# A two-layer decoder trunk on one core: keys times -1/8, attention parts at higher priority and further apart, the second half's row factors spread in one piece

## The chip, the cores and the metric

The kernel runs on one core of a Trainium2 chip. The metric is device time in microseconds (us), the median of several executions; lower is better. In the profile, PE is the engine of matmuls (TensorE) and PEld its weight loads, which overlap the matmuls; DVE (VectorE) does elementwise work and row reductions, ACT (ScalarE) activations and copies out of PSUM, POOL (GpSimd) further elementwise work, and SP issues the DMAs.

## The reference

One sequence of 1024 tokens, width 1024, goes through two layers. Layer 0 mixes by sliding-window attention, layer 1 by a gated recurrence (HGRN2); each layer has one wide input projection, a gate, an output projection and a norm on either side. The change concerns layer 0:

```python
h = rmsnorm(x, pre_norm_w)
q, k, v, z = split(h @ w_in + b_in, [1024, 1152, 1280])   # 16 query heads, 2 key heads, 64 wide
q, k = partial_rope(q), partial_rope(k)                   # rotates the first 16 of 64
# blocks of 128 queries against their own and the previous 128 keys:
s = einsum('bqhgd,bkhd->bhgqk', qi, ki) * 64 ** -0.5
s = where(valid, s, -inf)                                  # causal, at most 128 keys back
m = maximum(max(s, axis=-1), sink)                         # one learned sink per head
p = exp(s - m)
p = p / (sum(p, axis=-1) + exp(sink - m))
o = einsum('bhgqk,bkhd->bqhgd', p, v)
x = x + rmsnorm((o * silu(z)) @ w_out + b_out, post_norm_w)
```

## The kernel before

**Projections.** Every projection is computed as a sum of three matmuls: activations and weights are each split into a high part and the rest (the tiles `acth`/`actl` and `whi`/`wlo`), and `product` (L214) issues high times high, high times low and low times high, 128x512 each, into one PSUM tile. Eight products make a *unit*: 128 output columns for 512 tokens (`proj_feat`, L228). A weight piece arrives by DMA in `wraw`; POOL or ACT makes `whi` from it and DVE makes `wlo` (L179). There are ten places for split pieces, and one comes free when all its products are issued.

**What sets the order.** The products are the clock of the program: `later(d, f)` (L223) puts a piece of other work into a plan, to be issued d products from now, and `product` issues what is due. During attention, PE's instructions are kept in exactly this program order. The order on DVE, ACT, POOL and SP is chosen by a scheduler, from its own estimate of when operands are ready and from priorities: within `hp()` an instruction counts as 400 places earlier in the program than it stands. Each engine then runs its list strictly from front to back.

**Start.** Keys and values of token half 0, and the first query units, are computed before the normed activations exist in full: rows are scaled afterwards by factors that are turned into a 128x512 tile (`rb0`, `rb1`) by four PE transposes and one ACT copy (`spread`, tile `psr`). `first_scaled` does this for half 0 within the third unit (`ps2`), after its product 4. For half 1, `spread(rs1, rb1)` follows the fourth unit (`ps3`), then `q_unit(0, 0, 0)` projects and rotates the last query unit of half 0. `scaled_half` multiplies the second half's input `xt` by `rb1` (DVE) and splits it into `acth`/`actl`.

**Attention.** There are 32 steps, counted from 0: 2 key heads (g) x 8 blocks (b) x 2 (`par`, which four of the eight heads). Each step has three parts, put into the plan by the loop under `A0, AP, AT, AV = 25, 7.3, 11, 21`: step i's `scores` at product 25 + 7.3 i, its `turned` 11 products later, its `heads_out` 21 products later. The parts are called by `at_once`, within `hp()`. A step's chain through the engines is:

- `scores`: PE multiplies queries (`QS`, fetched by a DMA from DRAM) and keys (`KH`, `KL`) into two PSUM tiles `pss`; ACT copies the always-valid part to `sm` (L690), DVE copies the masked part over it with a predicate (L694, twice); column 129 of `sm` holds 8 times the sink. DVE takes each row's maximum (L698) into `st` and multiplies it by -1/8 (L699); ACT makes four exponentials (L701) with that as the bias and 1/8 as the scale, summing each row; DVE makes the reciprocals (L703) and scales `sm` by them (L704).
- `turned`: PE transposes `sm` in four matmuls (tile `pst`); ACT copies the high part to `pT` (L713), DVE makes the low part (L714), POOL zeroes what is outside the window (L720 to L728).
- `heads_out`: PE multiplies by the values (tile `pso`); ACT and DVE evict (L746, L747), and for g = 1 DVE multiplies into the gated tile `og` (L749).

Between these parts PE works off the list `fill`: the key unit of half 1, the value unit of half 1, the query units `q_unit(0, ct, 1)`, eight units `q_unit(1, ct, half)`, sixteen gate units (`z_unit`) and four units of the output projection. A query unit with `ct` = 0 is rotated (*rope*) with DVE operations at L423 to L425 and L427, the others take L430; both write a single-buffered tile `ql`, which a DMA moves to `qd` in DRAM. Before the output projection, `g_split` (L775) splits `og` for token half 0: ACT at L780, DVE at L781, the first four of the eight pieces in one go.

Of the kernel before, what the change touches and what calls it, by code (L numbers as in the profile page):

```python
# [27 lines left out]
NH = 16  # L28
HD = 64
EPS = 1e-6  # L30
NEG = -1.0e30


INV_FREQ = [float.fromhex(h) for h in (
# [55 lines left out]
def emit(tc, I, out):  # L90
# [9 lines left out]
    with top:  # L100
# [122 lines left out]
        def later(d, f, block=99):  # L223

            W["plan"].append((W["pos"] + d, f, block))
            W["plan"].sort(key=lambda e: e[0])

        def proj_feat(first, half, tag="mm", then={}):  # L228

            ps = mm(tag=tag)  # L230
            for k in range(NK):
                c = (k % 4) * P
                product(ps, k, weight(first, k // 4, c, c + P), act[k, half])
                used(first + k // 4)
                then.get(k, lambda: None)()
            return ps
# [48 lines left out]
        def bias(i):  # L285
            return cst[:, C_BIN + i:C_BIN + i + 1]
# [86 lines left out]
        def layer0():  # L373
# [26 lines left out]
            def q_first(g, ct):  # L400
                return 12 + 2 * ct if g else 2 * ct if ct else 8
# [35 lines left out]
            with pool("start", "right") as sp:  # L437
# [41 lines left out]
                with tc.high_priority(offset=1000):  # L479
# [50 lines left out]
                            sc.append(vsc if i == 0 else qp.tile([P, 512], F32, tag="th", bufs=2, name="sc"))  # L530
                            v.tensor_tensor(sc[i], first[i], rb0, op=ALU.mult)

                    ps2 = proj_feat(q_first(0, 2), 0, "s", {4: first_scaled})
                    split_next()
                    rs1 = [row_rstd(sp, rows[1][j], jkb) for j in range(4)]
                    cs3 = sines()
# [2 lines left out]
                    split_next()  # L539
                    ps3 = proj_feat(q_first(0, 3), 0, "s")  # L540
                    rb1 = sp.tile([P, 512], F32, name="rb1")
                    spread(rs1, rb1)
                    advance(W_K + 2)
                    for e in heads:
                        e.on = False
# [1 line left out]
                def k_unit(half):  # L547
                    cs = slice(half * 512, (half + 1) * 512)
                    ps = proj_feat(W_K, half)
                    with hp():  # L550
                        ps = scaled(ps, half)
                        kr = qp.tile([P, 512], F32, tag="th", bufs=2, name="kr") if half else ps
                        nc.scalar.activation(kr, ps, AF.Identity, bias=bias(0))
                    v.tensor_tensor(kf, kr, cosK[:, cs], op=ALU.mult)
                    for o in range(4):
                        s1, s2 = slice(32 * o, 32 * o + 8), slice(32 * (o ^ 1), 32 * (o ^ 1) + 8)
                        s3 = slice(64 * (o % 2), 64 * (o % 2) + 8)
                        v.tensor_tensor(tK[s1], kr[s2], sinT[s3, cs], op=ALU.mult)
                    v.tensor_tensor(kf, kf, tK, op=ALU.add)

                    def halves(kv):
                        kr = kf[64 * kv:64 * kv + 64]
                        for o in (0, 64):
                            nc.scalar.activation(KH[o:o + 64, kv, cs], kr, AF.Copy)
                            v.tensor_tensor(KL[o:o + 64, kv, cs], kr, KH[o:o + 64, kv, cs].bitcast(F32), op=ALU.subtract)

                    for kv in range(2):
                        if half:
                            def behind(kv):

                                with tc.issue_after(W["exp"].ins):
                                    halves(kv)
                            later(30 + 6 * kv, lambda kv=kv: behind(kv))
                        else:
                            halves(kv)

                def v_unit(half, ps=None, sc=None):
# [34 lines left out]
                        rest(VL, pl.rearrange("p (k d) -> p k d", k=2))  # L612

                    if half:
                        later(4, turned)
                        later(6, last_turned)
                    else:
                        turned()

# [1 line left out]
                q_unit(0, 1, 0, first[1], 0, sc[1])  # L621
                q_unit(0, 2, 0, ps2, 2)
                for_keys()
                nc.gpsimd.tensor_scalar(hbias, cst[:, C_BIN:C_BIN + 18], 0.5, 1.0, op0=ALU.mult, op1=ALU.mult)
                q_unit(0, 3, 0, ps3, 4)
                scaled_half(xt1, rb1, 1)
                q_unit(0, 0, 0, at=6)
                second_tables()
                k_unit(0)

            with pool("att", "right") as ap:
# [35 lines left out]
                def scores(g, b, par):  # L667
# [3 lines left out]
                    if par == 1 and (g, b) != order[-1]:  # L671
                        queries(*order[order.index((g, b)) + 1])
                    QS = QSs[g, b]

                    sms[g, b, par] = sm = ap.tile([P, 4, P + 1], F32, tag="sm", bufs=2, name="sm")
                    nc.gpsimd.tensor_scalar(sm[:, :, P:], cst[:, C_SINK + 8 * g + par:C_SINK + 8 * g + 8:2].unsqueeze(2),
                                            8.0, 1.0, op0=ALU.mult, op1=ALU.mult)
                    if b == 0:
                        nc.gpsimd.memset(sm[:, :, :P], NEG)
                    k0 = max(b - 1, 0) * P  # L680
                    nkk = (b + 1) * P - k0
                    for hp in range(2):
# [12 lines left out]
                                          mk.rearrange("p (u c) -> p u c", c=64).unsqueeze(1).to_broadcast([P, 2, 2, 64]), src)  # L695
                    st = ap.tile([P, 3, 4], F32, tag="st", bufs=4, name="st")
                    nm, dn, rd = (st[:, i, :] for i in range(3))
                    v.tensor_reduce(nm, sm, axis=AX.X, op=ALU.max)  # L698
                    v.tensor_scalar(nm, nm, -0.125, None, op0=ALU.mult)  # L699
                    for h in range(4):  # L700
                        W["exp"] = nc.scalar.activation(sm[:, h, :], sm[:, h, :], AF.Exp, bias=nm[:, h:h + 1], scale=0.125,  # L701
                                                        accum_out=dn[:, h:h + 1])
                    v.reciprocal(rd, dn)  # L703
                    v.tensor_tensor(sm[:, :, :P], sm[:, :, :P], rd.unsqueeze(2).to_broadcast([P, 4, P]), op=ALU.mult)  # L704
# [56 lines left out]
                order = [(g, b) for g in range(2) for b in range(8)]  # L761

                def at_once(f, *a):
                    with hp():
                        f(*a)


                A0, AP, AT, AV = 25, 7.3, 11, 21
                W["pos"] = 0
                for i, (g, b, par) in enumerate((g, b, par) for g, b in order for par in range(2)):  # L770
                    for d, f in ((0, scores), (AT, turned), (AV, heads_out)):
# [474 lines left out]
```

## Time and profile before

| what | value |
|---|---|
| time, median of 3 runs | 916.68 us (914.98 to 917.44) |
| time of the profiled execution | 916.49 us |
| its span (first to last instruction) | 914.8 us |
| TensorE clock granted, mean | 0.991 of full speed |
| PE busy | 881.2 us, 96% of the span |
| DVE busy | 573.2 us, 63% |
| ACT busy | 382.6 us, 42% |
| POOL busy | 337.5 us, 37% |

The profiled execution took 916.49 us against a span of 914.8 us: 1.7 us lie outside the span. Busy shares are means over stages that differ. In the listings a row of the timeline is: time from the span's start, duration, engine, line of the kernel, operation, output<-inputs, shape, and in brackets the idle time of the engine just ahead of this instruction, with what ended it. A row of the waits is: instruction group <- what released it, then the sum of the idle time, how often, and the longest. `L87` is the line of the helper that keeps an engine in program order; there the tile names tell what an instruction belongs to.

### The profile page before, as it was taken

The page shows a single profiled execution, that of the slowest core. Times are in us where ns is not written, and L with a number is a line of the kernel's source. Part 1 is how long each engine was busy: PE and PEld are TensorE (multiplying, and loading weights), DVE is VectorE, ACT ScalarE, POOL GpSimd, SP SyncE. Part 2 cuts the span into 40 slices and gives each one's busy share as a digit, 9 for nine tenths or more (in the row PEclk, how much of TensorE's full clock was granted, in tenths as well). Part 3 has the DMA queues.
Part 4 walks back from the last instruction along what each step waited for, and adds up shares of the span by engine and source line. Part 5 has one row for each costly group of instructions (what it writes and reads, how often), then busy time and mean ns, then how long its engine had stood idle before and what let it go on. Part 6 is the DMA issues. An engine that isn't in the chain of part 4 may idle for free.

```text
span 914.8 us, 14330 instructions
## 1 busy us (share of the span) xinstructions
PE 881.2 (96%) x5286; PEld 732.9 (80%) x5286; DVE 573.2 (63%) x940; ACT 382.6 (42%) x984; POOL 337.5 (37%) x498
## 2 busy tenths in 40 slices
PE   6989899999979999999999999999999999999996
PEld 5867788888867878878888888888888788888885
DVE  7898977778898535762368775246767924252243
ACT  5645566566566433543423341333334224252311
POOL 4423546556777502340054342115424433210011
PEclk9999999999999999999999999999999999999998
DMA  9766345423132124450311110120111003032053
GB/s 337 253 193 198 104 140 157 111 63 93 35 90 70 35 74 156 163 173 1 105 47 45 36 48 1 36 81 24 46 47 47 2 1 93 1 101 83 24 184 119
DMA packets 55767, 82.74 MB, mean 90 GB/s; under 512 B 5192, under 2 KB 25288, under 8 KB 55688
## 3 DMA queue, kind: packets, MB, share of 16 engines
q1 hardware_dynamic: 55408, 81.68, 28.7%
q8 instruction: 43, 0.70, 0.3%
q14 instruction: 36, 0.29, 0.1%
q10 hardware_dynamic: 280, 0.07, 0.0%
HBM read 63.01 MB, written 16.88 MB: 87 GB/s over the span
## 4 chain that ended last, share of the span: by engine, by line
PE 71%; DVE 10%; POOL 5%; issue 4%; ACT 2%; DMA 1%; POOLq 0%; SPq 0%; DVEq 0%; ACTq 0%
PE psmm L217 47%; PE psmm L87 12%; PE pss L87 2%; PE pso L87 2%; POOL rstd L255 2%; PE psk L1032 1%; PE pso L1045 1%; PE pst L87 1%; PE pso L1047 1%; ACT sm L701 1%; POOL ms L253 1%; DMA qd<-ql 1%; PE pst L1026 1%; PE pst L1059 1%; DVE wlo L179 1%
## 5 line engine op out<-in xcount | busy, mean ns | idle before, releaser
L217 PE MATMUL psmm<-whi,acth 128*128 128x512 f32 (+1 forms) x488 | 190.4, 391 | 1.0 <-DVE y L811 1.0
L217 PE MATMUL psmm<-wlo,acth 128*128 128x512 f32 (+1 forms) x488 | 188.7, 387 | 0.0
L217 PE MATMUL psmm<-whi,actl 128*128 128x512 f32 (+1 forms) x488 | 188.7, 388 | 0.0
L179 DVE TENSOR_TENSOR wlo<-wraw,whi 128x512 fp32r<-128x512 f32 x120 | 87.9, 744 | 92.4 <-ACT whi L178 85.9
L87 PE MATMUL psmm<-acth,whi 128*128 128x512 f32 x264 | 108.6, 411 | 3.0 <-ACT whi L87 1.7
L178 ACT ACTIVATE whi<-wraw 128x512 fp32r<-128x512 f32 x112 | 70.1, 631 | 93.6 <-PE psmm L217 65.5
L217 PEld LDWEIGHTS psmm<-whi,acth 128*128 128x128 f32 x488 | 91.7, 188 | 20.3 <-DVE y L811 1.8
L217 PEld LDWEIGHTS psmm<-whi,actl 128*128 128x128 f32 x488 | 91.7, 188 | 18.2
L217 PEld LDWEIGHTS psmm<-wlo,acth 128*128 128x128 f32 x488 | 91.8, 188 | 17.9
L87 PE MATMUL psmm<-actl,whi 128*128 128x512 f32 x264 | 105.2, 399 | 0.2 <-DVE actl L87 0.2
L87 PE MATMUL psmm<-acth,wlo 128*128 128x512 f32 x264 | 105.5, 399 | 0.0
L217 PE MATMUL psmm<-acth,whi 128*128 128x512 f32 x264 | 104.4, 396 | 0.2 <-DVE qf L885 0.2
L217 PE MATMUL psmm<-acth,wlo 128*128 128x512 f32 x264 | 103.5, 392 | 0.0
L217 PE MATMUL psmm<-actl,whi 128*128 128x512 f32 x264 | 103.4, 392 | 0.0
L701 ACT ACTIVATE sm<-sm,st 128x129 f32<-128x129 f32 x128 | 50.0, 393 | 39.6 <-DVE st L699 39.2
L893 POOL TENSOR_SCALAR gate<-gate,lbt 128x512 f32<-128x512 f32 x16 | 17.7, 1107 | 117.8 <-ACT gate L891 107.3
L87 PEld LDWEIGHTS psmm<-acth,whi 128*128 128x128 f32 x264 | 50.7, 192 | 11.4 <-ACT whi L87 2.0
L87 PEld LDWEIGHTS psmm<-acth,wlo 128*128 128x128 f32 x264 | 50.5, 191 | 11.7 <-DVE wlo L87 0.2
L217 PEld LDWEIGHTS psmm<-acth,whi 128*128 128x128 f32 x264 | 49.6, 188 | 11.1 <-DVE qf L885 0.9
L87 PEld LDWEIGHTS psmm<-actl,whi 128*128 128x128 f32 x264 | 50.7, 192 | 9.2 <-DVE actl L87 1.5
L217 PEld LDWEIGHTS psmm<-acth,wlo 128*128 128x128 f32 x264 | 49.6, 188 | 10.4
L217 PEld LDWEIGHTS psmm<-actl,whi 128*128 128x128 f32 x264 | 49.6, 188 | 9.7
(268 smaller groups left out, 1633.1 us busy)
## 6 DMA issues: line engine op xcount, KB each, us to landing
wraw<-in_w SPq DMA_DIRECT2D x132, 256.0 KB
QS<-qd SPq DMA_DIRECT2D x16, 512.0 KB
xr<-in_x SPq DMA_DIRECT2D x8, 512.0 KB
x1d<-xn SPq DMA_DIRECT2D x8, 512.0 KB
xr<-x1d SPq DMA_DIRECT2D x8, 512.0 KB
out_dram<-xn SPq DMA_DIRECT2D x16, 256.0 KB
o<-in_xt SPq DMA_DIRECT2D x8, 256.0 KB
xt<-in_x SPq DMA_DIRECT2D x4, 512.0 KB
```

Source lines behind the costliest of these rows:

```text
L87: return (lambda *a, **k: self.tc.keep_in_program_order(f(*a, **k))) if self.on else f
L178: nc.scalar.activation(hi, raw, AF.Copy)
L179: W["split_ins"][i] = v.tensor_tensor(lo, raw, hi.bitcast(F32), op=ALU.subtract)
L217: W["mm"] = pe.matmul(ps, a, b, start=(k == 0 and i == 0), stop=(k == NK - 1 and i == 2))
L253: keep(g.tensor_scalar(m, ms, eps, 1.0, op0=ALU.add, op1=ALU.mult))
L255: W["rstd"] = keep(g.tensor_tensor(r, m, nhalf[:, :width], op=ALU.pow))
L701: W["exp"] = nc.scalar.activation(sm[:, h, :], sm[:, h, :], AF.Exp, bias=nm[:, h:h + 1], scale=0.125, accum_out=dn[:, h:h + 1])
L893: nc.gpsimd.tensor_scalar(dst, dst, ol, lb, op0=ALU.mult, op1=ALU.add)
L1026: nc.tensor.transpose(pt[:, i, :], Y[:, c * P:(c + 1) * P], ident)
L1032: nc.tensor.matmul(pk[:, i, :], yn[:, c, :], vt[:, c, hc], start=True, stop=True)
L1045: nc.tensor.matmul(po[:, i, :], sc[:, c, :], vt[:, c, hc], start=True, stop=(c == 0))
L1047: nc.tensor.matmul(po[:, i, :], X[:, c * P:(c + 1) * P], S[:, c, :], start=False, stop=True)
```

## The change

- **Keys times -1/8.** The activation that adds the bias to the keys (of half 1, and of half 0) takes -1/8 as its scale, with the bias multiplied likewise (`hbias`, now filled in two pieces on POOL). Scores come out as minus the scaled scores. The fill for masked places becomes +1e30, the sink is multiplied by -1, the row reduction is a minimum, its result is used directly as the bias, and the exponentials take the scale -1. The 32 multiplications at L699 are gone.
- **Priority and distance.** `at_once` counts an attention part as 2000 places earlier instead of 400. `turned` follows `scores` after 13 products instead of 11, `heads_out` after 22 instead of 21.
- **Start.** `first_scaled` is issued after product 2 of `ps2`, not 4. The projection of `q_unit(0, 0, 0)` is issued ahead, right behind `ps3`, and `spread(rs1, rb1)` stands after its product 2, in PE's fixed order. In `v_unit(1)` the transposes come 7 and 12 products later, not 4 and 6.

```diff
-NEG = -1.0e30
+FAR = 1.0e30
...
-                    ps2 = proj_feat(q_first(0, 2), 0, "s", {4: first_scaled})
+                    ps2 = proj_feat(q_first(0, 2), 0, "s", {2: first_scaled})
...
-                    spread(rs1, rb1)
+                    ps0 = proj_feat(q_first(0, 0), 0, "mm", {2: lambda: spread(rs1, rb1)})
...
-                        nc.scalar.activation(kr, ps, AF.Identity, bias=bias(0))
+                        nc.scalar.activation(kr, ps, AF.Identity, bias=hbias[:, 0:1], scale=-0.125)
...
-                        later(4, turned)
-                        later(6, last_turned)
+                        later(7, turned)
+                        later(12, last_turned)
...
-                nc.gpsimd.tensor_scalar(hbias, cst[:, C_BIN:C_BIN + 18], 0.5, 1.0, op0=ALU.mult, op1=ALU.mult)
+                for c0, c1, c in ((0, 1, -0.125), (10, 18, 0.5)):
+                    nc.gpsimd.tensor_scalar(hbias[:, c0:c1], cst[:, C_BIN + c0:C_BIN + c1], c, 1.0, op0=ALU.mult, op1=ALU.mult)
...
-                q_unit(0, 0, 0, at=6)
+                q_unit(0, 0, 0, ps0, 6)
...
-                                            8.0, 1.0, op0=ALU.mult, op1=ALU.mult)
+                                            -1.0, 1.0, op0=ALU.mult, op1=ALU.mult)
                     if b == 0:
-                        nc.gpsimd.memset(sm[:, :, :P], NEG)
+                        nc.gpsimd.memset(sm[:, :, :P], FAR)
...
-                    v.tensor_reduce(nm, sm, axis=AX.X, op=ALU.max)
-                    v.tensor_scalar(nm, nm, -0.125, None, op0=ALU.mult)
+                    v.tensor_reduce(nm, sm, axis=AX.X, op=ALU.min)
...
-AF.Exp, bias=nm[:, h:h + 1], scale=0.125,
+AF.Exp, bias=nm[:, h:h + 1], scale=-1.0,
...
-                    with hp():
+                    with tc.high_priority(offset=2000):
                         f(*a)
...
-                A0, AP, AT, AV = 25, 7.3, 11, 21
+                A0, AP, AT, AV = 25, 7.3, 13, 22
```

In the changed kernel line numbers behind the keys are 1 to 3 higher: the row reduction of `scores` is L701, the exponentials L703, the reciprocal L705, the scaling L706.

On DVE, the softmax chain of step 3, counted from 0 (reduction, bias, reciprocal, scaling; the reduction at the head of the piece), stands among the rope of a query unit (tiles `qtB`, `qf`) and the eviction of other units. Before:

```order
L698 TENSOR_REDUCE st<-sm 128x4
L714 TENSOR_TENSOR pT<-pst,pT 128x512
L424 TENSOR_TENSOR qf<-qf,cosT 128x512
L699 TENSOR_SCALAR st<-st 128x4
L747 TENSOR_TENSOR o_136<-pso,ob 64x4x128
L425 TENSOR_TENSOR qf<-qf,qtB 128x512
L694 COPY_PREDICATED sm<-msk,pss 128x2x128
L397 TENSOR_TENSOR sc<-psmm,rb_176 128x512
L703 RECIPROCAL st<-st 128x4
L694 COPY_PREDICATED sm<-msk,pss 128x2x128
L704 TENSOR_TENSOR sm<-sm,st 128x4x128
```

And in the changed kernel, from the same reduction on:

```order
L701 TENSOR_REDUCE st<-sm 128x4
L423 TENSOR_TENSOR qtB<-qf,sinT 64x512 x2
L424 TENSOR_TENSOR qf<-qf,cosT 128x512
L705 RECIPROCAL st<-st 128x4
L425 TENSOR_TENSOR qf<-qf,qtB 128x512
L706 TENSOR_TENSOR sm<-sm,st 128x4x128
L716 TENSOR_TENSOR pT<-pst,pT 128x512
```

Between reduction and scaling stood nine other instructions, two of them of this chain (L699 and L703) and one the `pT` of step 2; now there are five, and that `pT` comes behind the scaling. The first half of the rope (L423), which stood ahead of the reduction, stands behind it.

Also on DVE, step 26's chain at the place where the first four pieces of `g_split` come in (`actl`). Before:

```order
L698 TENSOR_REDUCE st<-sm 128x4
L642 SCALAR_TENSOR_TENSOR th<-psmm,cst,th 128x512
L714 TENSOR_TENSOR pT<-pst,pT 128x512
L699 TENSOR_SCALAR st<-st 128x4
L781 TENSOR_TENSOR actl_0_121<-og_1031,acth_0_120 128x512
L781 TENSOR_TENSOR actl_0_125<-og_1031,acth_0_124 128x512
L781 TENSOR_TENSOR actl_0_129<-og_1031,acth_0_128 128x512
L781 TENSOR_TENSOR actl_0_133<-og_1031,acth_0_132 128x512
L179 TENSOR_TENSOR wlo_98<-wraw_100,whi_88 128x512
L703 RECIPROCAL st<-st 128x4
L704 TENSOR_TENSOR sm<-sm,st 128x4x128
```

And in the changed kernel:

```order
L701 TENSOR_REDUCE st<-sm 128x4
L179 TENSOR_TENSOR wlo_97<-wraw_103,whi_87 128x512
L751 TENSOR_TENSOR og_1028<-og_1028,ob 128x4x128
L644 SCALAR_TENSOR_TENSOR th<-psmm,cst,th 128x512
L705 RECIPROCAL st<-st 128x4
L706 TENSOR_TENSOR sm<-sm,st 128x4x128
L179 TENSOR_TENSOR wlo_98<-wraw_100,whi_88 128x512
L783 TENSOR_TENSOR actl_0_121<-og_1028,acth_0_120 128x512
L783 TENSOR_TENSOR actl_0_125<-og_1028,acth_0_124 128x512
L783 TENSOR_TENSOR actl_0_129<-og_1028,acth_0_128 128x512
L783 TENSOR_TENSOR actl_0_133<-og_1028,acth_0_132 128x512
L716 TENSOR_TENSOR pT<-pst,pT 128x512
```

The four splits stood between the reduction and the reciprocal and stand behind the scaling now; on ACT, likewise, the four exponentials of this step have moved from behind the four `acth` copies to ahead of them.

On DVE at the start, where the second half's input `xt` is scaled by `rb1` (`wlo` and `kw` are low parts of weights, `sc` is the scaled unit `ps3`, `VX` the values of half 0). Before:

```order
L397 TENSOR_TENSOR sc<-psmm,rb_176 128x512
L87 TENSOR_TENSOR wlo_99<-wraw_101,whi_89 128x512
L598 TENSOR_TENSOR VX<-pst,VX 128x8x64
L87 TENSOR_TENSOR kw_195<-wraw_102,kw_194 128x512
L430 SCALAR_TENSOR_TENSOR o_136<-sc,cst,o_136 128x512
L87 TENSOR_TENSOR kw_197<-wraw_103,kw_196 128x512
L87 TENSOR_TENSOR xt_206<-xt_206,rb_461 128x512 x3
```

And in the changed kernel:

```order
L87 TENSOR_TENSOR wlo_99<-wraw_101,whi_89 128x512
L397 TENSOR_TENSOR sc<-psmm,rb_176 128x512
L87 TENSOR_TENSOR kw_195<-wraw_102,kw_194 128x512
L87 TENSOR_TENSOR kw_197<-wraw_103,kw_196 128x512
L430 SCALAR_TENSOR_TENSOR o_136<-sc,cst,o_136 128x512
L87 TENSOR_TENSOR xt_206<-xt_206,rb_461 128x512 x3
L599 TENSOR_TENSOR VX<-pst,VX 128x8x64
```

`sc` has changed places with the `wlo` ahead of it, and the values' low part is made behind the first three pieces of `xt` instead of ahead of them.

On PE the number of matmuls is the same. Step i's transposes (`pst`) stand behind 13 products from its scores instead of 11, and its `pso` behind the scores of step i+3 without a product between, 9 products after its transposes instead of 10. Layer 1 is in the same order on every engine.

More of the change, by code (lines that the diff above doesn't have):

```diff
@@ L697, in scores @@
                     nm, dn, rd = (st[:, i, :] for i in range(3))
-                    v.tensor_reduce(nm, sm, axis=AX.X, op=ALU.max)
-                    v.tensor_scalar(nm, nm, -0.125, None, op0=ALU.mult)
+                    v.tensor_reduce(nm, sm, axis=AX.X, op=ALU.min)
                     for h in range(4):
-                        W["exp"] = nc.scalar.activation(sm[:, h, :], sm[:, h, :], AF.Exp, bias=nm[:, h:h + 1], scale=0.125,
+                        W["exp"] = nc.scalar.activation(sm[:, h, :], sm[:, h, :], AF.Exp, bias=nm[:, h:h + 1], scale=-1.0,
                                                         accum_out=dn[:, h:h + 1])
```

## The prediction

> **What bounds the kernel now.** I read four views in this order: busy shares, PE's waits, windows, and the timelines of PE and DVE around the waits. First, the busy shares and what PE waited for in the attention layer (sum in us, times, longest):
>
> ```profile
> PE 881.2 (96%) x5286; PEld 732.9 (80%) x5286; DVE 573.2 (63%) x940; ACT 382.6 (42%) x984; POOL 337.5 (37%) x498
> ...
> PE pst L87 <- DVE sm L704: 10.1, 5, 4.6
> ...
> PE psmm L87 <- DVE actl L87: 2.2, 2, 2.0
> ...
> PE pst L87 <- POOL vmid L591: 0.9, 1, 0.9
> ...
> PE pst L87 <- ACT acth L780: 0.5, 1, 0.5
> ```
>
> PE is the bound: with 96% busy and the same matmuls after the change, only idle PE time and slow clock can be won. The largest wait that the edits touch is the first: five times the transposes `pst` stood until DVE had scaled `sm`. On PE's timeline the five stand here (time, duration, instruction, idle before):
>
> ```profile
> 77.78 0.63 PE L87 MATMUL pst<-cst,sm 128*128 128x128 f32 x4 [1.16 <-DVE sm L704]
> ...
> 101.91 0.63 PE L87 MATMUL pst<-cst,sm 128*128 128x128 f32 x4 [3.45 <-DVE sm L704]
> ...
> 125.42 0.63 PE L87 MATMUL pst<-cst,sm 128*128 128x128 f32 x4 [0.29 <-DVE sm L704]
> ...
> 272.52 1.08 PE L87 MATMUL pst<-cst,sm 128*128 128x128 f32 x4 [4.61 <-DVE sm L704]
> ...
> 290.13 0.63 PE L87 MATMUL pst<-cst,sm 128*128 128x128 f32 x4 [0.58 <-DVE sm L704]
> ```
>
> They form two groups, steps 0 to 6 (77 to 126 us) and steps 26 to 28 (272 to 291 us). Between them PE never waits here. The windows (length, then busy time and count of PE, PEld, DVE, ACT, POOL; granted clock; DMA share; GB/s) say what is special there:
>
> ```profile
> 80.00:100.00 20.00, 18.46 (x98) 15.32 (x96) 17.65 (x30) 13.07 (x39) 9.43 (x17) 1.00 0.42 125
> 100.00:120.00 20.00, 18.09 (x88) 15.27 (x89) 19.51 (x37) 12.45 (x34) 11.91 (x18) 0.91 0.44 129
> 260.00:280.00 20.00, 15.39 (x72) 12.75 (x71) 17.80 (x29) 11.63 (x29) 14.26 (x19) 0.83 0.31 84
> 280.00:300.00 20.00, 18.91 (x98) 15.41 (x97) 19.23 (x34) 14.57 (x44) 14.95 (x22) 1.00 0.24 67
> 140.00:160.00 20.00, 20.00 (x109) 17.08 (x108) 14.81 (x28) 13.74 (x42) 12.54 (x23) 1.00 0.60 169
> ```
>
> In both groups DVE is nearly full (17.65 to 19.51 of 20 us); in the middle it is at 14.81 and PE runs through. So DVE's load decides, and within it the order: how late `sm` comes after the scores. And twice the clock falls as well (0.91 and 0.83). Matmuls of one kind, before a long wait and behind it:
>
> ```profile
> 78.94 0.40 PE L87 MATMUL psmm<-acth,whi 128*128 128x512 f32 x1
> 79.18 0.39 PE L87 MATMUL psmm<-actl,whi 128*128 128x512 f32 x1
> ...
> 103.31 0.59 PE L87 MATMUL psmm<-actl,whi 128*128 128x512 f32 x1
> ...
> 104.12 0.63 PE L87 MATMUL psmm<-acth,whi 128*128 128x512 f32 x1
> 104.55 0.63 PE L87 MATMUL psmm<-actl,whi 128*128 128x512 f32 x1
> ...
> 106.68 0.43 PE L87 MATMUL psmm<-acth,whi 128*128 128x512 f32 x1
> ...
> 276.82 0.63 PE L87 MATMUL psmm<-acth,wlo 128*128 128x512 f32 x1
> ```
>
> They normally follow each other by 0.23 us (a product of three takes 0.69), behind the waits of 3.45 and 4.61 us by 0.43. From 103.3 to 106.7 us stand seven such matmuls and two half as long, 3.4 us instead of 8 x 0.23 = 1.8: 1.5 us lost, rounded. From 272.5 to 277.8 the transposes, nine products' matmuls and two of `pso` lose about 2.3. No such stretch follows the waits of 1.16 and 0.58 us.
>
> **The change part by part.**
>
> *Two more products ahead of the transposes* give 2 x 0.69 = 1.4 us more between scores and `pst`, at every step, for nothing. They cost DVE, ACT and POOL no instruction.
>
> *The multiplication at L699* goes:
>
> ```profile
> L699 DVE TENSOR_SCALAR st<-st 128x4 f32<-128x4 f32 x32 | 9.6, 300 | 0.4
> ```
>
> 32 x 0.30 = 9.6 us of DVE, of which about 7 x 0.30 = 2.1 fall in the first group and 2.4 in the last eight steps; elsewhere PE does not wait and they are worth nothing. The keys' scale rides in an activation that is there anyway; the reduction is the same shape with another operation, and I price both at nothing (a row of reductions takes 0.69 us; to lose or win more than a tenth of that per step there is no reason).
>
> *The priority.* Here is DVE's chain at step 3, ahead of the 3.45 us wait, and at step 26, ahead of the 4.61 us wait:
>
> ```profile
> 94.31 1.60 DVE L423 TENSOR_TENSOR qtB<-qf,sinT 64x512 f32<-64x512 f32 x2
> 95.94 0.69 DVE L698 TENSOR_REDUCE st<-sm 128x4 f32<-128x516 f32 x1
> ...
> 101.09 0.68 DVE L704 TENSOR_TENSOR sm<-sm,st 128x512 f32<-128x512 f32 x1
> ...
> 263.01 0.68 DVE L179 TENSOR_TENSOR wlo<-wraw,whi 128x512 fp32r<-128x512 f32 x1
> 263.60 0.90 DVE L749 TENSOR_TENSOR og<-og,ob 128x512 f32<-128x512 f32 x1
> 264.43 0.68 DVE L698 TENSOR_REDUCE st<-sm 128x4 f32<-128x516 f32 x1
> 265.02 0.73 DVE L642 SCALAR_TENSOR_TENSOR th<-psmm,cst,th 128x512 f32<-128x512 f32 x1
> ...
> 267.14 3.36 DVE L781 TENSOR_TENSOR actl<-og,acth 128x512 fp32r<-128x512 f32 x4
> ...
> 271.68 0.69 DVE L704 TENSOR_TENSOR sm<-sm,st 128x512 f32<-128x512 f32 x1
> ```
>
> Step 26: in the new order the reduction comes ahead of `wlo` and `og`, so it can start at 263.0; then wlo 0.6, og 0.8, th 0.7 (start to start), reciprocal 0.2, scaling 0.7: `sm` ready at about 263.0 + 0.6 + 3.0 = 266.6. The exponentials, four at 0.39, end before the reciprocal. PE was free for this `pst` at 272.52 - 4.61 = 267.9, two products later at 269.3. The wait goes, with 2.7 us to spare, because the four splits (3.36 us) now stand behind the scaling. Step 3: the reduction can start at 94.3; reduction 0.6, L423 1.6, L424 0.6, reciprocal 0.2, L425 0.6, scaling 0.7: ready at 98.6. PE was free at 101.91 - 3.45 = 98.5, now at 99.9: this wait goes too.
>
> What is late next? **First group.** DVE's work has not gone. From 80 to 120 us it has 40 - 17.65 - 19.51 = 2.8 us unused, and PE wants to run 1.16 + 3.45 + 0.29 + 1.5 = 6.4 us faster from there to 126. The rope that step 3 overtakes is paid by step 4. Going through the new order step by step with the durations of these rows, I find `sm` of step 4 about 2.0 us late, two waits of 0.3 to 0.5 near step 0 and 3, and about 1.2 near steps 6 and 7, where DVE stands twice for the single `ql` buffer. That is some 3.9, a gain of 2.5. By the sum it would be 1.4 (two products) + 2.1 (L699) = 3.5. I take 3.0; ends 0 and 6.4. **Last group.** DVE has room ahead of it, and the splits at step 26 push later work by 3.4 us; going through steps 26 to 31, `sm` stays 2 us or more ahead of PE. The gain is the two waits 4.61 + 0.58, the clock 2.3, the `acth` wait 0.5: 8.0. But `pT` of step 25 now stands behind the splits, and `pso` follows `pst` after nine products, not ten (next rival); I take 0.5 off: 7.5, ends 4 and 8.
>
> *The start.* Two rows bear on the spread in one piece, DVE's `wlo` and PE's wait for `actl` of the second half; a third bears on the transposes of `v_unit`:
>
> ```profile
> 34.87 1.08 DVE L87 TENSOR_TENSOR wlo<-wraw,whi 128x512 fp32r<-128x512 f32 x1 [1.52 <-POOL whi L87]
> ...
> 50.09 0.50 PE L87 MATMUL psmm<-actl,kw 128*128 128x512 f32 x1 [2.02 <-DVE actl L87]
> ...
> 67.04 0.19 PEld L87 LDWEIGHTS pss<-KH,QS 128*128 128x128 f32 x1 [0.36 <-issue]
> ```
>
> `rb1` comes about one unit's part earlier, but in the new order `sc`, which used the time before 34.87, stands behind this `wlo`, about 0.6 us on DVE's path, and `VX` (0.7) moves behind the scaling of `xt`: nearly nothing is left at 50.09. Ends: 1.0 won, 0.6 lost; I take 0.2 lost. The transposes of `v_unit` get 3 x 0.69 = 2.1 us more cover, so their wait of 0.9 for `vmid` goes; but the first scores behind them wait for `QS`, which the last row shows as already late (0.36), and `tw` transfers come ahead of it on SP's queue. I count 0, ends 0.9 won and 1 lost. The extra POOL instruction for `hbias` is a small one, once, long before attention: 0, at worst 0.3, the length of an L699.
>
> **Sum:** 3.0 + 7.5 - 0.2 = 10.3 us off the profiled 916.5 us: **906.2, say 906**. The median of the runs is 916.7, 0.2 above the profiled one, so the same number serves.
>
> [...] The rows: half speed behind 3.45 and 4.61 us of idle PE, none behind 1.16. [...]
>
> **The rivals.**
>
> *A. DVE is simply full in the first group* and the wait moves whole from step 3 to steps 4 and 5, clock loss with it: gain there 0, total 7.5 - 0.2 = 7.3, 909. If the waits of the last group shrink by the two products alone, 1.4 each, and the clock still falls, the total is about 1.4 + 1.4 + 1.4 + 0.6 = 5: 911.5. For it: 2.8 us of unused DVE against 6.4 wanted. Against: the splits leave the chain in the written order.
>
> *B. `pso` waits for `pT`.* POOL's last two masks after the splits, step 25's:
>
> ```profile
> 268.98 0.99 POOL L726 TENSOR_SCALAR_AFFINE_SELECT pT<-pT 128x512 fp32r<-128x512 f32 x1
> 269.93 1.09 POOL L728 TENSOR_SCALAR_AFFINE_SELECT pT<-pT 128x512 fp32r<-128x512 f32 x1
> ```
>
> From DVE's `pT` to the end of L728 it is about 3.6 to 5 us. In the new order that `pT` comes some 5.7 us behind `pst`, and `pso` about 9.5: between 0.2 us to spare and 1.2 late, once or twice. With the same at step 3, some 2.5 in all instead of my 0.5: 908.
>
> *C. Slower: DVE stands at the reciprocal.* DVE takes its list strictly in order. If the reciprocal follows the reduction closely, DVE stands until ACT has made four exponentials:
>
> ```profile
> DVE st L703 <- ACT sm L701: 22.0, 22, 1.8
> ...
> 89.67 0.18 DVE L703 RECIPROCAL st<-st 128x4 f32<-128x4 f32 x1 [1.21 <-ACT sm L701]
> ```
>
> In the new order steps 1, 2 and 25, among others, have a single instruction between the two. If all 15 steps of the two full stretches stand 1.2 us, that is 18 us of DVE, less 4.5 for L699 and some 3 that stand there already: 10.5 us more on an engine that is full, and nothing is won: 927. It decides against the gain from 10.3 / 15 = 0.7 us of new standing a step. Against it: at steps 3 and 26 three instructions or more stand between, longer than the exponentials, and I find only 4 to 5 us of such standing. [...]
>
> *D. The change does not do what it says:* the spread in one piece brings nothing. That is in the forecast already, by DVE's order.
>
> **How the numbers follow.** Forecast (903 to 909): 0.45. A and B, alone or together (909 to 914): 0.23. Better, with all waits gone (916.5 - 6.4 - 8 - 1 = 901): 0.10. Gains and losses cancel, 914 to 919, where about 0.3% (2.75 us) is what a measurement of this kernel can tell from no change: 0.12. C, 919 and above: 0.10. Range 901 to 914.5 leaves 0.2 out. Faster 0.78, same 0.12, slower 0.10.
>
> **What would show it.** PE's waits: `pst` for `sm` down from 10.1 to 2 to 4 us, none of them near step 26, and one of about 2 at step 4. The clock at 1.00 in the windows around 270 and 105 us. `pso` waiting for POOL under 1 us; more is B. The reciprocal's wait of 22.0 us about the same; above 35 is C. The wait for `actl` near 50 us still about 2. I am wrong if a wait of over 3.4 us remains in either group, or if DVE is no fuller than before between 80 and 120 us while PE still waits.

## The result, and the profile after

The changed kernel takes 909.47 us (median of four runs, 908.42 to 910.11) against 916.16 us before (914.98 to 917.44): a ratio of 0.9926, with a 95% interval of 0.9908 to 0.9943. That is 6.7 us faster; forecast were 10.3. The time lies in the range, but not in the forecast's own band (903 to 909): it stands 0.5 us inside the band that was given to the rivals A and B. The profiled execution took 909.15 us with a span of 907.4. Of all the runs below, one execution, of the kernel with the start edits alone, took 3120 us against 914 to 921 in its nine others, and is left out of that kernel's ratio.

First what PE waits for in the changed kernel (group <- releaser: sum in us, times, longest), with its busy share:

```profile
PE 880.0 (97%) x5286; PEld 733.6 (81%) x5286; DVE 567.5 (63%) x908; ACT 382.4 (42%) x984; POOL 328.4 (36%) x499
...
PE psmm L87 <- DVE actl L87: 3.6, 2, 3.4
PE pst L87 <- DVE sm L706: 1.8, 1, 1.8
PE pso L87 <- POOL pT L730: 1.8, 3, 1.2
...
PE pss L87 <- DVE sm L697: 1.2, 1, 1.2
```

The transposes waited 10.1 us for `sm`, and now 1.8. New are waits of `pso` for POOL (1.8), of the scores `pss` for DVE's copies (1.2), and more for the second half's `actl` (3.6 instead of 2.2). On PE's timeline they stand here:

```profile
51.73 0.80 PE L87 MATMUL psmm<-actl,kw 128*128 128x512 f32 x1 [3.37 <-DVE actl L87]
52.32 1.05 PE L87 MATMUL psmm<-acth,kw 128*128 128x512 f32 x2
...
109.37 0.63 PE L87 MATMUL pst<-cst,sm 128*128 128x128 f32 x4 [1.79 <-DVE sm L706]
...
126.86 0.39 PE L87 MATMUL pss<-KH,QS 128*128 128x256 f32 x1 [1.25 <-DVE sm L697]
...
271.42 0.73 PE L87 MATMUL pso<-pT,VX 128*128 128x512 f32 x2 [1.24 <-POOL pT L730]
```

The wait of 3.37 us at the start is followed by matmuls at half speed (two in 1.05 us), and the trace records half clock from 50.98 to 57.81 us. In the windows the slow clock is gone from both attention groups, while DVE is as full as before:

```profile
80.00:100.00 20.00, 20.00 (x106) 16.93 (x106) 17.09 (x32) 14.93 (x44) 8.18 (x15) 1.00 0.49 146
100.00:120.00 20.00, 18.21 (x102) 15.40 (x100) 18.86 (x34) 11.99 (x39) 11.63 (x19) 1.00 0.43 122
...
260.00:280.00 20.00, 18.76 (x103) 15.92 (x102) 19.28 (x31) 15.41 (x44) 14.62 (x21) 1.00 0.31 88
280.00:300.00 20.00, 19.45 (x100) 15.91 (x100) 18.37 (x29) 12.46 (x41) 15.02 (x24) 1.00 0.27 84
```

Where the time came from, read off PE's timelines as the difference (after minus before) of the starts of the same scores `pss`: step 0 stands at +1.5 us, step 10 at -2.0, step 27 at -2.6, step 31 at -9.1. From step 3 on, each step's `pso` follows the scores instead of preceding them, which flatters the later differences by some 0.7. So the start lost 1.5, the first group won 2.8, the last group 6.5 and the stretch between them 0.5: 8.3, of which 7.4 are left in the span.

Step 26 on DVE shows the order that the forecast read off the lists; the splits `actl` stand behind the scaling:

```profile
258.61 0.69 DVE L701 TENSOR_REDUCE st<-sm 128x4 f32<-128x516 f32 x1
259.22 0.92 DVE L179 TENSOR_TENSOR wlo<-wraw,whi 128x512 fp32r<-128x512 f32 x1
260.06 1.10 DVE L751 TENSOR_TENSOR og<-og,ob 128x512 f32<-128x512 f32 x1
261.08 0.74 DVE L644 SCALAR_TENSOR_TENSOR th<-psmm,cst,th 128x512 f32<-128x512 f32 x1
261.74 0.16 DVE L705 RECIPROCAL st<-st 128x4 f32<-128x4 f32 x1
261.94 1.81 DVE L706 TENSOR_TENSOR sm<-sm,st 128x512 f32<-128x512 f32 x1
...
264.27 2.91 DVE L783 TENSOR_TENSOR actl<-og,acth 128x512 fp32r<-128x512 f32 x4
```

`sm` is ready at 263.75; its transposes start at 267.25 without waiting. What the trace can't say is which of the edits put this right. Twelve kernels were run for that.

### The profile page after: what moved, and what is told of

It is laid out like the page before. It is cut to its first block, busy times and chain, and to the rows that moved or that the text cites. A ratio compares the mean times of both kernels' runs of the same rounds, so it can differ in the third digit from the quotient of the medians.

```text
span 907.4 us, 14278 instructions
## 1 busy us (share of the span) xinstructions
PE 880.0 (97%) x5286; PEld 733.6 (81%) x5286; DVE 567.5 (63%) x908; ACT 382.4 (42%) x984; POOL 328.4 (36%) x499
## 4 chain that ended last, share of the span: by engine, by line
PE 77%; DVE 8%; POOL 4%; issue 3%; DMA 2%; ACT 2%; SPq 0%; DVEq 0%; POOLq 0%; ACTq 0%
PE psmm L217 47%; PE psmm L87 16%; PE pss L87 2%; PE pso L87 2%; POOL rstd L255 2%; PE psk L1034 1%; PE pso L1047 1%; PE pst L87 1%; PE pso L1049 1%; DMA qd<-ql 1%; POOL ms L253 1%; PE pst L1028 1%; PE pst L1061 1%; DMA csd<-cs 1%; PE psd L985 1%
## 5 line engine op out<-in xcount | busy, mean ns | idle before, releaser
L703 ACT ACTIVATE sm<-sm,st 128x129 f32<-128x129 f32 x128 | 50.0, 393 | 45.2 <-DVE st L701 45.1
L217 PEld LDWEIGHTS psmm<-acth,wlo 128*128 128x128 f32 x256 | 48.1, 188 | 10.1
```

Of the source, the lines that this page charges most:

```text
L217: W["mm"] = pe.matmul(ps, a, b, start=(k == 0 and i == 0), stop=(k == NK - 1 and i == 2))
```

## The experiments

In every run the ratio is to the kernel before on the same chip, with its 95% interval.

### One part undone at a time

**Start undone.**

```diff
-{2: first_scaled}
+{4: first_scaled}
...
-ps0 = proj_feat(q_first(0, 0), 0, "mm", {2: lambda: spread(rs1, rb1)})
+spread(rs1, rb1)
...
-later(7, turned)
-later(12, last_turned)
+later(4, turned)
+later(6, last_turned)
```

> The changed kernel with its start edits undone (first_scaled after product 4, rb1's transposes behind the fourth unit, q_unit(0, 0, 0) projected in its old place, v_unit's transposes 4 and 6 products later). Theory: the trace after shows the first scores 1.5 us later than before (68.57 against 67.08 us), behind a wait of 3.37 instead of 2.02 us for the second half's actl, and that is what the start part costs: 1.5 us faster than the changed kernel's 909.5, so 908, the wait near 50 us back at 2.0, and the first scores near 67.1. Rival: DVE is full from there to 121 us, so what the start wins is lost again at the next step: 909.5, same time at step 8.

Measured: 910.98 us, ratio 0.9935 (0.9913 to 0.9956); no gain shows, which is what the rival said. The start is quicker in its trace: scores of step 0 at 67.65 instead of 68.57. Steps 0 and 4 then wait for `sm`, where the changed kernel waited 0 and 1.79 us:

```profile
79.30 0.63 PE L87 MATMUL pst<-cst,sm 128*128 128x128 f32 x4 [0.69 <-DVE sm L706]
...
110.28 0.63 PE L87 MATMUL pst<-cst,sm 128*128 128x128 f32 x4 [2.50 <-DVE sm L706]
```

What PE gains ahead of a full DVE is gone by the scores of step 2 (81.15 against 81.22), and step 4 costs it more than in the changed kernel.

**Priority undone.**

```diff
-with tc.high_priority(offset=2000):
+with hp():
```

> The changed kernel with attention parts at priority 400 again. Theory: PE, DVE and ACT get the very same lists with 400 as with 2000; only two masks on POOL and the order of DMAs on SP differ. So 909.5, within 1 us, and no wait for sm near step 26: the two other parts moved the splits behind the softmax. Rival (the step of my prediction): the priority does it, and the wait of some 2 us or more at step 26 returns: 912 or more.

Measured: 908.73 us, ratio 0.9905 (0.9884 to 0.9926), the changed kernel's own time. No wait for `sm` near step 26. The lists of PE, DVE and ACT are the same with 400 as with 2000, so the priority has no part in the gain that this measurement can show.

**Distances undone.**

```diff
-AT, AV = 25, 7.3, 13, 22
+AT, AV = 25, 7.3, 11, 21
```

> The changed kernel with distances 11 and 21 again. Theory: the distance carries most of the gain, since it also lets the scheduler place the four splits behind the softmax; with 11 and 21 they stand between reduction and reciprocal as before. Waits of pst for sm over 3 us return at step 26 and at step 3 or 4: 915 to 917. Rival: keys and priority carry it, the distance is only 1.4 us twice: 911 to 912.

Measured: 913.46 us, ratio 0.9964 (0.9952 to 0.9977): between the two expectations. The waits for `sm` are back, shorter than before the change:

```profile
134.79 0.63 PE L87 MATMUL pst<-cst,sm 128*128 128x128 f32 x4 [2.31 <-DVE sm L706]
272.06 0.63 PE L87 MATMUL pst<-cst,sm 128*128 128x128 f32 x4 [2.38 <-DVE sm L706]
```

At steps 0 and 3 stand 1.16 and 0.98 us more, and 1.99 at step 4, which the profile puts down to ACT, although `sm` was ready only 0.15 us before these transposes start.

**Keys undone.**

```diff
-v.tensor_reduce(nm, sm, axis=AX.X, op=ALU.min)
+v.tensor_reduce(nm, sm, axis=AX.X, op=ALU.max)
+v.tensor_scalar(nm, nm, -0.125, None, op0=ALU.mult)
```

with the keys, the fill, the sink and the exponentials as before.

> The changed kernel with the keys unscaled: maximum, the multiplication by -1/8 and the scales as before. Theory: 0.30 us more on a full DVE at each of steps 0 to 7 and 25 to 31, and two of the splits stand between reduction and reciprocal again: 911 to 912.5, the wait of step 4 longer by about 1.2 us. Rival: the multiplication lies in the time in which DVE stands for the exponentials anyway: 909.5.

Measured: 916.33 us, ratio 1.0000 (0.9989 to 1.0010). Both expectations missed, by almost 4 us or more: without the keys' scale no gain of the change is left that shows. In its trace the first group waits 1.16 and 2.11 us at steps 3 and 4 (put down to ACT, with `sm` ready 0.15 us before). In the last group a wait has moved to step 27, where the changed kernel has none:

```profile
282.79 1.09 PE L87 MATMUL pst<-cst,sm 128*128 128x128 f32 x4 [3.29 <-DVE sm L706]
```

DVE's rows of this step show the longer chain. Without the keys' scale:

```profile
273.76 0.67 DVE L700 TENSOR_REDUCE st<-sm 128x4 f32<-128x516 f32 x1
...
276.82 1.26 DVE L701 TENSOR_SCALAR st<-st 128x4 f32<-128x4 f32 x1
...
280.81 0.16 DVE L705 RECIPROCAL st<-st 128x4 f32<-128x4 f32 x1
...
281.55 1.09 DVE L706 TENSOR_TENSOR sm<-sm,st 128x512 f32<-128x512 f32 x1
```

and with it, in the changed kernel:

```profile
269.56 0.67 DVE L701 TENSOR_REDUCE st<-sm 128x4 f32<-128x516 f32 x1
...
272.65 0.17 DVE L705 RECIPROCAL st<-st 128x4 f32<-128x4 f32 x1
272.86 1.84 DVE L706 TENSOR_TENSOR sm<-sm,st 128x512 f32<-128x512 f32 x1
```

From the start of the reduction to the end of the scaling it takes 8.9 us with the multiplication and 5.1 without. The multiplication starts 3.1 us after the reduction does, since it stands in DVE's list behind work of others, and lasts 1.26 us here (half of the 32 last 0.17 or less); the exponentials cannot start before its result. The two DVE lists differ in many more places than this one instruction, though, so the 3.8 us between them are not the multiplication's alone.

### One part alone

These are the kernel before with the lines of the change that belong to one part: for the keys and for the start those of the diffs above, taken the other way round, for the distances this:

```diff
-A0, AP, AT, AV = 25, 7.3, 11, 21
+A0, AP, AT, AV = 25, 7.3, 13, 22
```

> The kernel before with the keys' scale alone. What undoing showed: without the keys' scale the changed kernel gives back all 7 us, without the distances 4. Theory (the two work together: DVE's time from the scale, the splits' place from both): alone the scale wins what the changed kernel has left without the distances, 916.6 - 913.5 = 3, so 913 to 914; the splits still stand inside step 26's chain and the wait there is 2 to 3 us, short enough for the clock. Rival (the scale alone does it): 910.

Measured, keys alone: 912.71 us, ratio 0.9958 (0.9936 to 0.9980): 4 us won, near the 3 of the theory and not the 6.7 of the rival. The wait at step 26 is 2.61 us in its trace, and against the expectation slow matmuls follow it: those of one kind start 0.42 to 0.43 us apart from 271.81 to 273.09 us, and 0.23 from 273.42 on.

> The kernel before with the distances 13 and 22 alone. Theory: nothing is won alone, 916 to 917, since DVE stays as full and the time is lost a step later (as in the changed kernel without the keys' scale, where a wait of 3.3 us came up at step 27); rival: two products more are 1.4 us at each of the two groups, 913 to 914.

Measured, distances alone: 916.42 us, ratio 0.9993 (0.9981 to 1.0006): nothing that shows. In its trace step 4 waits 2.10 us and step 27 3.27.

> The kernel before with the start edits alone. Theory (the start part costs 1 to 1.5 us, by the first scores' time in the traces): 917.5 to 918. Rival (it shifts waits about, and DVE takes them up until step 4): 916.5.

Measured, start alone: 918.51 us, ratio 1.0011 (0.9995 to 1.0028): anything from 0.5 us won to 2.6 lost, so theory and rival are not told apart. Its trace does not show DVE taking up the delay: the scores of step 0 stand 2.0 us later than before the change, those of step 31 2.9 us.

So by the medians the keys' scale is worth 4.0 us alone and the distances 0.3. The changed kernel won 6.7, and the kernel with its start undone, which has both, 5.6: some 1.3 to 2.4 us belong to neither alone, and with intervals of about 2 us on either side that figure is rough.

### Is it DVE's time?

The multiplication is put back into the changed kernel (`st` gets a fourth row for it), but nobody reads its result:

```diff
 v.tensor_reduce(nm, sm, axis=AX.X, op=ALU.min)
+v.tensor_scalar(st[:, 3, :], nm, -0.125, None, op0=ALU.mult)
```

> The changed kernel with a multiplication of the row minima by -1/8 put back on DVE at each step, right behind the reduction, whose result nobody reads: 32 times some 0.3 us of DVE, while PE, POOL and SP keep their lists, DVE and ACT theirs but for five swaps of neighbours, and the exponentials need not wait for it. Theory A (DVE's time): 0.3 us at each of 15 full steps come back, 4 to 5 us of it: 913 to 914. Theory B (the order: the scale is worth 7 us because it lets the scheduler put the splits and pT elsewhere): 909.5 to 911.

Measured: 909.64 us, ratio 0.9921 (0.9899 to 0.9943), against the 913 to 914 of theory A. Off the chain, the multiplication costs nothing that shows. Step 27 in this kernel, where the multiplication is L702:

```profile
268.65 0.67 DVE L701 TENSOR_REDUCE st<-sm 128x4 f32<-128x516 f32 x1
...
271.14 0.39 DVE L702 TENSOR_SCALAR st<-st 128x4 f32<-128x4 f32 x1
...
272.03 0.16 DVE L706 RECIPROCAL st<-st 128x4 f32<-128x4 f32 x1
272.23 1.57 DVE L707 TENSOR_TENSOR sm<-sm,st 128x512 f32<-128x512 f32 x1
```

It comes 2.5 us behind the reduction, as late as ever, and the reciprocal stands right behind `pT` 0.9 us later: the exponentials had been running meanwhile. How much work was added has to be read with care. The 32 multiplications last 8.4 us in sum, but rows overlap: DVE is busy 571.9 us against 567.5 in the changed kernel, 4.4 more. And its waits at the reciprocal fall from 17.1 to 12.9 us, so about as much standing went as work came. The run shows that the multiplication is free off the chain, and not that time on DVE is worth nothing everywhere.

The same reading for all steps, from the start of the row reduction to the end of the scaling on DVE's timeline, means in us of one profiled execution:

| kernel | steps 0 to 7 | steps 24 to 31 | all 32 | multiplication in the chain | median, us |
|---|---|---|---|---|---|
| before | 5.4 | 5.8 | 4.9 | yes | 916.2 |
| keys undone | 6.1 | 5.8 | 5.2 | yes | 916.3 |
| distances alone | 6.0 | 5.8 | 5.2 | yes | 916.4 |
| keys alone | 4.7 | 4.5 | 4.1 | no | 912.7 |
| multiplication beside | 4.8 | 4.5 | 4.0 | no | 909.6 |
| changed kernel | 4.5 | 4.4 | 3.9 | no | 909.5 |
| distances undone | 4.5 | 4.5 | 4.1 | no | 913.5 |
| before, splits told to wait (next section) | 5.4 | 5.6 | 4.9 | yes | 920.8 |
| keys alone, splits told to wait (next section) | 4.7 | 4.4 | 4.1 | no | 915.1 |

With the multiplication in it (0.27 to 0.30 us in the mean), the chain is longer by 0.8 us in the mean of all steps (before against keys alone) to 1.2 (keys undone against the changed kernel), and by 1.3 to 1.4 in the last group. There the instruction itself lasts 0.35 to 0.48 us in the mean; the rest goes with the place that it takes in a full list. The mean chain alone does not set the time: with the distances undone it is nearly that of the changed kernel, and the kernel is 4 us slower.

### Is it the place of the splits?

The four splits that stand in step 26's chain read `og`, the second half of the gated tile: they are the last four of the eight pieces, not the first four, as the text ahead of the prediction has it. They are told to stand behind a softmax scaling (`W["scale"]`, the last one issued so far) on DVE's list, in the kernel before and in the one with the keys alone:

```diff
+with tc.issue_after(W["scale"].ins) if not half and p >= 4 else ExitStack():
     nc.scalar.activation(hi, o, AF.Copy)
     v.tensor_tensor(lo, o, hi.bitcast(F32), op=ALU.subtract)
```

> The kernel before with one thing changed: the four late splits of token half 0 (actl) are told to stand behind a softmax scaling on DVE's list, so they leave step 26's chain; the multiplication, the distances and the priority stay. Theory (order): the wait of 4.6 us at step 26 and the slow clock behind it go, 4 to 6.5 us are won: 910 to 912.5. Rival (DVE is simply full in the last group): a wait of 3 us or more comes up at step 27 or 28, as in the changed kernel without the keys' scale: 915 to 916.5.

Measured, in the kernel before: 920.76 us, ratio 1.0044 (1.0027 to 1.0061), slower than both expectations. The wait at step 26 shrinks to 2.62, and a larger one comes two steps later:

```profile
270.81 0.63 PE L87 MATMUL pst<-cst,sm 128*128 128x128 f32 x4 [2.62 <-DVE sm L704]
...
292.92 1.09 PE L87 MATMUL pst<-cst,sm 128*128 128x128 f32 x4 [6.82 <-DVE sm L704]
```

DVE's rows of that step 28:

```profile
283.97 0.68 DVE L698 TENSOR_REDUCE st<-sm 128x4 f32<-128x516 f32 x1
...
286.69 0.15 DVE L699 TENSOR_SCALAR st<-st 128x4 f32<-128x4 f32 x1
...
290.13 0.75 DVE L642 SCALAR_TENSOR_TENSOR th<-psmm,cst,th 128x512 f32<-128x512 f32 x1 [1.16 <-POOL th L638]
290.80 0.17 DVE L703 RECIPROCAL st<-st 128x4 f32<-128x4 f32 x1
```

Again the multiplication stands 2.7 us behind the reduction, and the reciprocal behind an instruction that waits for POOL.

> The keys' scale alone, distances 11 and 21, and the four splits told to stand behind a scaling as in the run before. Theory (order): the wait of 2.6 us at step 26 goes, 912.7 less 2.5 to 3 is 910, about what the whole change gives. Rival: the splits crowd a later step, 912.5.

Measured, with the keys alone: 915.10 us, ratio 0.9977 (0.9964 to 0.9991). By the medians that is 2.4 us slower than the keys alone, by the ratios 1.7, with intervals that overlap; the 910 of the theory is out of the interval. The wait of step 26 goes, and one comes up at step 28:

```profile
288.03 1.09 PE L87 MATMUL pst<-cst,sm 128*128 128x128 f32 x4 [3.23 <-DVE sm L704]
```

That theory fell twice: with this one group of instructions out of step 26's chain, a wait as long or longer came up at step 28.

### Further apart still

```diff
-A0, AP, AT, AV = 25, 7.3, 13, 22
+A0, AP, AT, AV = 25, 7.3, 13, 23
```

> The changed kernel with heads_out 23 products behind the scores instead of 22. Theory: the three waits of pso for POOL's masks in the last group (1.8 us in the trace after) have 0.7 us more cover and shrink to 0.6: 908.3. Rival: DVE and POOL are full there, the cover is used up by a step later: 909.5.

Measured: 909.76 us, ratio 0.9916 (0.9897 to 0.9936), the rival's. The `pso` waits are gone from its trace, and scores wait for DVE's copies instead (0.44 and 0.29 us near 287).

And with 14 and 23:

```diff
-A0, AP, AT, AV = 25, 7.3, 13, 22
+A0, AP, AT, AV = 25, 7.3, 14, 23
```

> The changed kernel with distances 14 and 23. Theory: step 3's chain is shorter in this order (the two halves of the rope stand behind it), and one more product covers step 4's wait of 1.8 us: 908 to 908.5. Rival: DVE sets the pace from 80 to 120 us whatever the distance: 909.5.

Measured: 909.44 us, ratio 0.9925 (0.9909 to 0.9942), again the rival's. The wait at step 4 is gone from its trace, and waits of 0.93 and 1.49 us come up at steps 5 and 6. None of the kernels beats the changed one by more than the measurement can tell.

## Why the prediction was right, and where it was not

**What bounds the kernel:** right. PE's idle time in two groups and the slow clock behind it were what there was to win, and they were won there.

**The last group** was forecast at 7.5 us and gave 6.5. The waits of 4.61 and 0.58 us and the slow clock went, as the rows said. The term that was too small is rival B's: `pso` waits for `pT`, taken at 0.5, measured at 1.24 + 0.36 + 0.18 = 1.8 in the trace.

**The first group** was forecast at 3.0 and gave 2.8. The leftover wait at step 4 was forecast at 2.0 and is 1.79, and one of about 1.2 near steps 6 and 7 came at step 8's scores with 1.25. The sum of the prediction has no slow clock behind the wait at step 4. That was an estimate: no run shows a length up to which a wait costs no clock. The trace before has 1.00 in the windows from 48 to 56 us, behind the wait of 2.02 us for `actl`, and half clock behind 3.45. The 1.79 us were not followed by slow matmuls (granted clock 1.00 from 109 to 115 us). That was partly luck: behind a wait of 2.07 us (multiplication beside) at the same step, matmuls of one kind start 0.43 us apart instead of 0.23.

**The start** was forecast at 0.2 lost; in the profiled execution it is 1.5. The wait for `actl` grew from 2.02 to 3.37 and brought half speed with it, where I expected about 2 and none. DVE's rows show that the order I read was right (`wlo`, then `sc`) and cost little; what was late is a table that the rope waits for, ahead of the last three `actl`:

```profile
48.29 0.68 DVE L423 TENSOR_TENSOR qtB<-sc,sinT 64x512 f32<-64x512 f32 x1 [0.73 <-DMA sinT<-csd]
50.13 0.69 DVE L423 TENSOR_TENSOR qtB<-sc,sinT 64x512 f32<-64x512 f32 x1 [1.16 <-DMA sinT<-csd]
```

Before, the only such wait was 0.39. In the new order SP issues a weight fetch and one more query write ahead of the tables' loads (at 38.96 and 40.26 us), because the projection was moved ahead; that this is what delays the table was not tried. I had counted DVE's order for that step and not the DMAs that move along with it. The loads of the tables themselves are issued only 0.2 us later than before (`cosT` at 43.26 instead of 43.08). With the start undone no gain shows, and with the start alone the interval leaves a loss of up to 2.6 us open, so what the start costs in the median is not settled. The profiled execution is 7.3 us faster (916.49 to 909.15), the sum said 10.3: of these 3 us the start has 1.3, the last group 1.0, the first 0.2, and 0.9 are lost at the end of attention and behind it, against 0.5 won between the groups, which the sum did not have.

**The reason, however, was put in the wrong place.** "The priority" was the step under which I read the new order, and the priority does nothing that shows: with 400 the lists of PE, DVE and ACT are the same, and the time is too. "The multiplication at L699 goes" was priced at 32 x 0.30 us of DVE, 2.1 and 2.4 of it useful; "two more products" at 1.4 us each time. Measured, DVE is busy only 5.7 us less (573.2 to 567.5), since its rows overlap; 4.4 us of such work put back cost nothing that shows (multiplication beside). The whole of the keys' edit is worth 4 us alone and 7 with the other edits in place. My sum came out in the range because I took the order of the finished lists and followed it row by row. The parts that were argued from the edits were wrong, and that they came near the row-by-row result for the first group (3.5 against 2.5) was chance.

What carries the gain is shown as far as this: undoing the keys' scale loses all of it, undoing the distances more than half, undoing the priority or the start nothing that shows. The chain from reduction to scaling is 0.8 us and more shorter only in kernels where the exponentials do not wait for a second DVE instruction, and with two more products ahead of the transposes `sm` was late at one step only (1.79 us at step 4). **Open** is how much of the 7 us is the shorter wait itself and how much the different list that the scheduler makes from it; the DVE lists of the changed kernel and of the one with the keys undone differ in more than a hundred places, and the multiplication in the chain under the changed kernel's list was not tried.

**Rivals.** A held in part: a wait of 1.8 us stayed at step 4. B held in part too: the waits for POOL of 1.8 us are over the 1 us that was its sign. C did not come: the reciprocal's waits fell from 22.0 to 17.1 us. D fits: the start edits, of which the spread in one piece is one, gave no gain that shows, alone or undone; the spread by itself was not tried.

## What to carry to other kernels

On an engine that works its list in order and is as full as DVE here (17.65 to 19.51 of 20 us in the windows of the two groups before), a small instruction in a dependency chain can cost more than its length: kernels with 0.3 us of work in the chain had chains 0.8 to 1.4 us longer here, and the same work beside the chain cost nothing that shows. So fold such a step into one that is there anyway, and look at slack and chain together, since more slack alone gave nothing that shows. And test each part of a change by undoing it: here one of the four (the priority) left the lists of the three busiest engines as they were, and another (the start) moved waits about without a gain that shows.

## What the runs showed of the hardware

The length of a single wait does not tell in these traces whether slow clock follows. In the kernel with keys alone and splits told to wait, a PE wait of 2.00 us was followed by matmuls of one kind 0.43 us apart instead of 0.23, and the granted clock falls to 0.50 (fields of the last three rows as in the windows above, the busy time of PE first):

```profile
133.22 1.09 PE L87 MATMUL pst<-cst,sm 128*128 128x128 f32 x4 [2.00 <-DVE sm L704]
133.96 0.78 PE L87 MATMUL psmm<-acth,whi 128*128 128x512 f32 x1
134.53 0.63 PE L87 MATMUL psmm<-actl,whi 128*128 128x512 f32 x1
134.96 0.63 PE L87 MATMUL psmm<-acth,wlo 128*128 128x512 f32 x1
...
130.00:132.00 2.00, 1.21 (x6) 0.66 (x4) 0.49 (x1) 0.99 (x3) 1.39 (x3) 1.00 0.68 211
132.00:134.00 2.00, 0.78 (x5) 0.81 (x5) 1.90 (x5) 0.00 (x0) 0.00 (x0) 0.80 0.49 151
134.00:136.00 2.00, 2.00 (x7) 1.61 (x6) 1.89 (x4) 0.51 (x3) 0.20 (x1) 0.50 0.35 110
```

In the kernel before with the splits told to wait, 2.62 us were not, and the clock stays at 1.00:

```profile
271.74 0.40 PE L87 MATMUL psmm<-acth,wlo 128*128 128x512 f32 x1
271.97 0.40 PE L87 MATMUL psmm<-acth,whi 128*128 128x512 f32 x1
...
270.00:272.00 2.00, 1.19 (x8) 1.09 (x9) 2.00 (x5) 2.00 (x5) 0.59 (x2) 1.00 1.00 319
272.00:274.00 2.00, 2.00 (x11) 1.66 (x10) 2.00 (x4) 0.81 (x2) 1.75 (x3) 1.00 0.42 80
274.00:276.00 2.00, 2.00 (x15) 1.81 (x15) 1.93 (x5) 1.72 (x7) 1.86 (x3) 1.00 0.26 97
```

Both kinds also stand in one trace: with the distances undone, matmuls of one kind start 0.42 to 0.43 us apart behind the wait of 2.38 us at 272.06, and 0.23 behind that of 2.31 at 134.79. And in the kernel before, the clock stays at 1.00 behind 2.02 us:

```profile
50.09 0.50 PE L87 MATMUL psmm<-actl,kw 128*128 128x512 f32 x1 [2.02 <-DVE actl L87]
...
50.00:52.00 2.00, 1.91 (x8) 1.38 (x8) 2.00 (x6) 0.00 (x0) 0.55 (x1) 1.00 0.71 245
52.00:54.00 2.00, 0.67 (x3) 0.42 (x3) 2.00 (x6) 1.26 (x2) 1.32 (x4) 1.00 0.55 189
54.00:56.00 2.00, 2.00 (x11) 1.63 (x10) 0.87 (x4) 1.99 (x4) 0.00 (x0) 1.00 0.29 89
```

What sorts these waits is not shown here. The rows that the prediction read had half speed behind 3.45 and 4.61 us and none behind 1.16; the waits above lie between, and the shortest of them with slow clock behind it is 2.00 us.
